# Scan rows of x and B: TensorE transposes replaced by VectorE 32x32 transposes and a round trip through DRAM

## The chip, the cores and the metric

The kernel runs on one core of one Trainium2 chip. The metric is device microseconds of one execution, from the first to the last instruction and what lies around them, as the median of the runs. Five engines work side by side, each with a queue of its own that it takes in order: TensorE (PE, with its weight loads PEld), VectorE (DVE), ScalarE (ACT), GpSimd (POOL) and SyncE (SP), which here only issues DMAs. ScalarE issues DMAs too; 16 DMA engines carry them all.

## The reference, cut to what matters

One step of a hybrid decoder layer for 336 tokens: 16 meta tokens, 256 prompt tokens and 8 sequences of 8 sample tokens.

```
h = rms_norm(x);  proj = h @ w_in                  # 2048 -> 18496 columns
xs, B, C = silu(conv4(proj[xBC]) + b)              # 4096 + 8*128 + 8*128 columns
dt = softplus(proj[dt] + dt_bias);  log_a = -dt * exp(a_log)
# per chunk of the scan, per group g of 8 heads:
cb   = C_i . B_j                                   # (i, j) tokens of a chunk
y    = sum_j cb * decay(i, j) * dt_j * x_j  +  C_i . h * exp(acum_i)
h    = exp(acum_end) * h + sum_j (to_end_j * dt_j * x_j) B_j
y = group_rms_norm((y + d_skip * xs) * silu(z)) @ w_ssd_out
# beside it a gated short convolution; both gated, @ w_o, + x, rms_norm
```

The scan contracts over tokens, so x and B are needed with tokens on the partitions ("rows"), while the projection and the conv leave them with channels on the partitions and tokens along them.

## The kernel before

All matmuls of the projections run as three products of a split: a weight block of 128x1024 is loaded on SyncE's queue (L92), ScalarE rounds it into `whi` (L94), VectorE makes the rest `wlo` (L96), and TensorE takes 8 steps of `whi` against both halves of the activations (L111, L112) and 8 of `wlo` against the upper half (L115). That is 24 matmuls a block; a unit (`unit`, `proj`) is two blocks into one bank of `pj`. Loads, `whi` and `wlo` have three buffers each, `pj` and `ms` banks two.

After the first part (norm, short convolution) the eight groups of the scan follow. While group g is scanned, the weight units of its neighbours are run, and the scan is woven between them: `weave` runs the units in the order z of g (four units), out projection of g−1 (eight units of one block), conv of g+1 (six units), and after each unit takes as many of the 23 steps of the generator `ssd(g)` as its share of the work. So each group has a z stage, an out stage (gate units in group 0 and at the end) and a conv stage, and the end of one conv stage is the start of the next z stage. A scheduler then fixes the order within each engine's queue from the program and its own estimates. It also hands out eight DMA semaphores in turn, over both queues, and lets a DMA wait until the holder before it has landed.

`conv_tile` evacuates a unit on ScalarE (`pad`, L462, L463), starts the conv there (L469), continues on VectorE (L471, three steps), takes the tanh on ScalarE (`cth`, L474) and writes the tile on VectorE (L475, L476): B (`BT`), C (`CT`) and four tiles of x (`xs`), in that order. `cacc` has two buffers.

In `ssd`, `rows(c)` for the three chunks (128, 128 and 80 tokens) makes the rows on TensorE: four transposes of `xs` and one of `BT` against the identity into two `ms` banks, and C.B of the chunk as one matmul in fp32 (recorded as two). VectorE multiplies the x rows by dt (`xdt`, L539), ScalarE and VectorE split the B rows (`bt`, L546, L547), VectorE masks C.B (`cbm`, L551). `decay(c)` makes the decay matrix in `W` (loaded from DRAM by L527), `weights(c)` multiplies it by `cbm` and makes `xe` on GpSimd (L568), `halve(c)` splits `xe`, `state(c)` is the update of the running state on TensorE (L585). The sample part updates `h` from the banks that L713 fills (VectorE, L716), and the group's normalising (`ms_r`, `ys`, `yh`, `yl`; L700 to L728) falls into the conv stage.

```
S = [{} for _ in range(NG)]
for _ in conv_units(0, S[0]):
    pass
for g in range(NG):
    parts = [(z_units(g, S[g]), 4, 2)]
    ...
    weave(parts, ssd(g, S[g]))
```

## Time and profile before

| | us |
|---|---|
| median of 3 runs | 1823.98 (1823.73 to 1824.63) |
| profiled execution, its own time | 1824.75 |
| its span, first to last instruction | 1823.0 |
| PE busy | 1814.9 |
| DVE busy | 1147.7 |
| ACT busy | 828.8 |
| POOL busy | 389.4 |
| granted TensorE clock | 1.00 |

A row of the timeline is: start, length, engine, line, operation, out<-in, shapes, count, and in brackets the idle time before it and what ended it. Neighbouring equal rows are merged. Matmuls overlap, so their cost is read from start to start. The view of a line or tile gives the shortest, median and longest duration in ns. A DMA issue appears as a row of the issuing queue (SPq, ACTq) and does not count as busy.

### The profile page before, as it was taken

The page shows a single profiled execution, that of the slowest core. Times are in us where ns is not written, and L with a number is a line of the kernel's source. Part 1 is how long each engine was busy: PE and PEld are TensorE (multiplying, and loading weights), DVE is VectorE, ACT ScalarE, POOL GpSimd, SP SyncE. Part 2 cuts the span into 40 slices and gives each one's busy share as a digit, 9 for nine tenths or more (in the row PEclk, how much of TensorE's full clock was granted, in tenths as well). Part 3 has the DMA queues.
Part 4 walks back from the last instruction along what each step waited for, and adds up shares of the span by engine and source line. Part 5 has one row for each costly group of instructions (what it writes and reads, how often), then busy time and mean ns, then how long its engine had stood idle before and what let it go on. Part 6 is the DMA issues. An engine that isn't in the chain of part 4 may idle for free.

```text
span 1823.0 us, 32410 instructions
## 1 busy us (share of the span) xinstructions
PE 1814.9 (100%) x13006; PEld 1798.0 (99%) x13006; DVE 1147.7 (63%) x1696; ACT 828.8 (45%) x1269; POOL 389.4 (21%) x398
## 2 busy tenths in 40 slices
PE   9999999999999999999999999999999999999998
PEld 9999999999999999999999999999999999999998
DVE  7745544444543335668587787877778777776544
ACT  6433333333333334645656354564546545343543
POOL 0000000000000001253162433524334252400012
PEclk9999999999999999999999999999999999999999
DMA  7444444444444446457566574665656657476553
GB/s 254 146 151 150 150 149 149 145 152 151 156 152 159 160 162 227 149 178 240 163 201 223 177 246 150 208 215 178 238 157 211 206 169 249 153 243 213 184 175 129
DMA packets 117286, 331.33 MB, mean 182 GB/s; under 512 B 20944, under 2 KB 37904, under 8 KB 117136
## 3 DMA queue, kind: packets, MB, share of 16 engines
q1 hardware_dynamic: 116272, 327.89, 55.9%
q8 instruction: 102, 1.67, 0.4%
q10 hardware_dynamic: 864, 1.38, 0.2%
q14 instruction: 48, 0.39, 0.1%
HBM read 296.34 MB, written 32.88 MB: 181 GB/s over the span
## 4 chain that ended last, share of the span: by engine, by line
PE 96%; DMA 2%; ACT 1%; DVE 1%; issue 0%; POOLq 0%; POOL 0%; SPq 0%; ACTq 0%; DVEq 0%
PE pj L111 30%; PE pj L112 30%; PE pj L115 29%; PE yb L650 2%; DMA wraw<-w 1%; PE ms L636 1%; PE pj L219 1%; PE yb L585 1%; PE pj L862 1%; ACT whi L94 0%; PE ms L534 0%; ACT W L559 0%; PE ms L219 0%; DMA ssms<-h 0%; PE yb L713 0%
## 5 line engine op out<-in xcount | busy, mean ns | idle before, releaser
L111 PE MATMUL pj<-hx,whi 128*128 128x320 f32 (+3 forms) x2880 | 864.4, 312 | 0.0
L112 PE MATMUL pj<-hx,whi 128*128 128x320 f32 (+3 forms) x2880 | 860.6, 311 | 0.0
L96 DVE TENSOR_TENSOR wlo<-wraw,whi 128x1024 fp32r<-128x1024 f32 x470 | 596.8, 1270 | 413.9 <-ACT whi L94 206.8
L94 ACT ACTIVATE whi<-wraw 128x1024 fp32r<-128x1024 f32 x470 | 496.7, 1057 | 768.0 <-PE pj L112 628.1
L111 PEld LDWEIGHTS pj<-hx,whi 128*128 128x128 f32 x2880 | 540.7, 188 | 4.6 <-ACT pad L462 1.7
L112 PEld LDWEIGHTS pj<-hx,whi 128*128 128x128 f32 x2880 | 541.5, 188 | 0.1
L115 PE MATMUL pj<-hx,wlo 128*128 128x320 f32 (+3 forms) x2880 | 485.4, 310 | 0.0
L115 PEld LDWEIGHTS pj<-hx,wlo 128*128 128x128 f32 x2880 | 440.6, 188 | 0.0
L111 PE MATMUL pj<-yh,whi 128*128 128x320 f32 x512 | 153.5, 311 | 1.2 <-ACT zs L503 0.9
L112 PE MATMUL pj<-yl,whi 128*128 128x320 f32 x512 | 152.3, 309 | 0.0
L596 POOL TENSOR_TENSOR h<-h,decS 128x512 f32<-128x512 f32 x64 | 76.4, 1227 | 147.5 <-PE ms L636 147.5
L111 PEld LDWEIGHTS pj<-yh,whi 128*128 128x128 f32 x512 | 96.2, 188 | 3.1 <-ACT zs L503 1.4
L112 PEld LDWEIGHTS pj<-yl,whi 128*128 128x128 f32 x512 | 96.3, 188 | 0.6
L115 PE MATMUL pj<-yh,wlo 128*128 128x320 f32 x512 | 95.8, 309 | 0.0
L242 POOL COPY SCS<-up 128x2 f32<-128x2 f32 x16 | 18.2, 1139 | 359.2 <-DVE up L236 329.0
L744 DVE TENSOR_TENSOR yan<-yan,pj 128x320 f32<-128x320 f32 x112 | 54.2, 485 | 62.9 <-PE pj L115 61.3
L471 DVE SCALAR_TENSOR_TENSOR cacc<-pad,V,cacc 128x360 f32<-128x360 f32 (+1 forms) x144 | 89.5, 621 | 2.0
L464 POOL COPY pad<-cs 128x24 f32<-128x24 f32 x48 | 56.2, 1172 | 126.6 <-DVE cacc L471 115.5
L115 PEld LDWEIGHTS pj<-yh,wlo 128*128 128x128 f32 x512 | 80.4, 188 | 0.0
L111 PE MATMUL pj<-vhi,whi 128*128 128x320 f32 x256 | 75.5, 308 | 0.0
L112 PE MATMUL pj<-vlo,whi 128*128 128x320 f32 x256 | 75.5, 308 | 0.0
L465 POOL COPY cs<-pad 128x3 f32<-128x3 f32 x48 | 45.0, 938 | 82.5 <-ACT pad L462 82.0
(286 smaller groups left out, 1721.7 us busy)
## 6 DMA issues: line engine op xcount, KB each, us to landing
wraw<-w SPq DMA_DIRECT2D x346, 512.0 KB, 3.9
wraw<-wso SPq DMA_DIRECT2D x64, 512.0 KB, 3.5
wraw<-wsc SPq DMA_DIRECT2D x32, 512.0 KB, 3.8
h<-h0T SPq DMA_DIRECT2D x32, 512.0 KB, 4.9
ssms<-h SPq DMA_DIRECT2D x32, 512.0 KB, 4.2
wraw<-wo SPq DMA_DIRECT2D x32, 512.0 KB, 3.9
xq_d<-xe SPq DMA_DIRECT2D x16, 320.0 KB, 3.4
W<-ac_d SPq DMA_DIRECT2D x8, 576.0 KB, 6.4
```

The source lines that it names most:

```text
L94: latest["act"] = nc.scalar.activation(hi[:, :n], raw[:, :n], AF.Copy).ins
L96: latest["dve"] = nc.vector.tensor_tensor(lo[:, :n], raw[:, :n], fb(hi[:, :n]), sub).ins
L111: nc.tensor.matmul(out, w, xh(k0 + k), start=first and k == 0, stop=False)
L112: nc.tensor.matmul(out, w, xl(k0 + k), start=False, stop=False)
L115: latest["pe"] = nc.tensor.matmul(out, w, xh(k0 + k), start=False, stop=last and k == nk - 1).ins
L219: nc.tensor.matmul(pu[i][:, :T - t0], w[:, o:o + P], x[:, k, t0:], start=k == 0 and j == 0, stop=k == 15 and j == 2)
L464: nc.gpsimd.tensor_copy(smp[:, :, 0:3], cs[:, 1:9, :])
L465: nc.gpsimd.tensor_copy(cs[:, 0, :], pad[:, 272:275])
L471: nc.vector.scalar_tensor_tensor(acc[:, i0:], pad[:, i0 + k:360 + k], col(V_CW, 4 * j + k), acc[:, i0:], mult, add)
L596: nc.gpsimd.tensor_tensor(split(h0[b]), split(h0[b]), bc(hv(decS[:, b, :], g), [P, 8, HP]), mult)
L650: nc.tensor.matmul(yb[q * HP:(q + 1) * HP, t, t0:t0 + n], x[:, h * HP:(h + 1) * HP], w[:, h, :], start=i == 0, stop=i == 3)
L744: nc.vector.tensor_tensor(ya[:, m, :TV], ya[:, m, :TV], pp[:, :TV], add)
```

## The change

The conv tile now also makes its rows. After a tile of B or x is written, VectorE transposes it in blocks of 32x32 (320 tokens, then the last 32) back into the tile's `cacc`. That leaves token 32b+q of channel block a on partition 32a+q. Four DMAs a tile, one for each 32 partitions, write it to DRAM (`xr_d`, two buffers by group) as rows by token: 32 x 11 pieces of 32 numbers each. They are put in a list and issued on ScalarE's queue (`flush`) after the first conv step of the next tile, or after the evacuation of the first z unit. `load(c)` reads the rows back with eight DMAs a group on SyncE's queue. `rows` is gone: C.B of the three chunks is made in one visit (`cross`), and `rows_in(c)` multiplies and splits the loaded rows. `decay(1)` comes a step earlier, `weights(0)` and `rows_in` a step later than `rows` and `weights(0)` stood.

The diff:

```diff
--- before.py
+++ after.py
@@ -28,6 +28,7 @@
 DUM = 14
 WARM = 10
 NSTEP = 23
+XR = 352
 
 C_ID, C_U, C_M1, C_UQ, C_M1Q, C_ONE = 0, 128, 272, 400, 480, 560
 C_SEG = 688
@@ -60,6 +61,7 @@
     sg_d = dr.tile([KT, P, TV], F32, name="sg_d")
     xq_d = [dr.tile([80, 4, 512], F32, name=f"xq_d{i}") for i in range(2)]
     bq_d = [dr.tile([80, 4, P], F32, name=f"bq_d{i}") for i in range(2)]
+    xr_d = [dr.tile([XR, 640], F32, name=f"xr_d{i}") for i in range(2)]
 
     V = keep.tile([P, V_ALL], F32, name="V")
     CR = keep.tile([P, C_ALL], F32R, name="CR")
@@ -454,7 +456,13 @@
         nc.gpsimd.memset(CZ, 0.0)
         czs = CZ.rearrange("p (s i w) -> p s i w", s=2, w=40)
 
-        def conv_tile(src, j, t0, out, cs):
+        pend = []
+
+        def flush():
+            while pend:
+                nc.scalar.dma_start(*pend.pop(0))
+
+        def conv_tile(src, j, t0, out, cs, rows=None):
             pp = proj(src, t0)
             pad = pads[npad[0] % 2]
             npad[0] += 1
@@ -467,6 +475,7 @@
             i0 = META if t0 else 0
             acc = pb.tile([P, 360], F32, name="cacc")
             nc.scalar.activation(acc[:, i0:], pad[:, i0:360], AF.Identity, bias=col(V_CB, j), scale=col(V_CW, 4 * j))
+            flush()
             for k in range(1, 4):
                 nc.vector.scalar_tensor_tensor(acc[:, i0:], pad[:, i0 + k:360 + k], col(V_CW, 4 * j + k),
                                                acc[:, i0:], mult, add)
@@ -477,19 +486,27 @@
                 out[:, 272:].rearrange("p (b t) -> p b t", t=8),
                 th[:, 272:360].rearrange("p (b t) -> p b t", t=11)[:, :, 3:11], 1.0,
                 acc[:, 272:360].rearrange("p (b t) -> p b t", t=11)[:, :, 3:11], add, mult)
+            if rows is not None:
+                nc.vector.transpose(acc[:, :320], out[:, :320])
+                nc.vector.transpose(acc[:, 320:XR], out[:, T - 32:])
+                to, c = rows
+                for a in range(0, P, 32):
+                    pend.append((to.rearrange("(b q) c -> q b c", q=32)[:, :, c + a:c + a + 32],
+                                 acc[a:a + 32, :XR].rearrange("p (b f) -> p b f", f=32)))
 
         def conv_units(g, st):
             cs = pb.tile([P, 6, 9, 3], F32, name="cs")
             nc.sync.dma_start(cs, convst[:, g])
+            to = xr_d[g % 2]
             BT = st["BT"] = pb.tile([P, T], F32, name="BT")
-            conv_tile(w1[64 + g], 32 + g, 0, BT, cs[:, 4])
+            conv_tile(w1[64 + g], 32 + g, 0, BT, cs[:, 4], (to, 512))
             yield
             CT = st["CT"] = pb.tile([P, T], F32, name="CT")
             conv_tile(w1[72 + g], 40 + g, 12, CT, cs[:, 5])
             yield
             xs = st["xs"] = pb.tile([P, 4, T], F32, name="xs", tag=f"xs{g % 2}", bufs=1)
             for t in range(4):
-                conv_tile(w1[32 + 4 * g + t], 4 * g + t, 0, xs[:, t, :], cs[:, t])
+                conv_tile(w1[32 + 4 * g + t], 4 * g + t, 0, xs[:, t, :], cs[:, t], (to, P * t))
                 yield
             nc.sync.dma_start(convo[:, g], cs)
 
@@ -501,6 +518,7 @@
                 th = pb.tile([P, 360], F32, name="cth", bufs=1)[:, :TV]
                 nc.scalar.activation(th, pz, AF.Tanh, scale=0.5)
                 nc.scalar.activation(z[:, :TV], pz, AF.Copy)
+                flush()
                 nc.vector.scalar_tensor_tensor(z[:, :TV], th, 1.0, z[:, :TV], add, mult)
                 st["zs"].append(z)
                 yield
@@ -518,7 +536,7 @@
             xw = free[:, :1024].rearrange("p (i n) -> p i n", n=512)
             h0, h0t = [], []
             ys = pb.tile([P, 4, T], F32, name="ys", bufs=1)
-            W, xdt, xe, bt, cbm, hst = ([None] * 3 for _ in range(6))
+            W, xdt, xe, cbm, hst = ([None] * 3 for _ in range(5))
             W[0], W[1] = (pb.tile([P, 8, PX], F32, name="W")[:, :, :n] for n in (P - META, PX))
             W[2] = pb.tile([P, 8, 80], F32, name="W2", bufs=1)
             E = pb.tile([P, 8, PX], F32, name="E", bufs=1)
@@ -527,29 +545,37 @@
                 nc.sync.dma_start(w[:r], ac_d[c][8 * g:8 * g + 8, :].partition_broadcast(r))
             NT, TGT = (P - META, PX, 80), (META, P, 2 * P)
 
-            def rows(c):
-                (t0, n), m = CH[c], NT[c]
-                pp = ps.tile([P, 512], F32, name="ms")
-                for t in range(4):
-                    nc.tensor.transpose(pp[:n, t * P:t * P + P], xs[:, t, t0:t0 + n], ident)
+            bt = [pb.tile([P, 2, P], F32R, name="bh0", bufs=1), free[:, 1024:1280].rearrange("p (i n) -> p i n", n=P),
+                  pb.tile([P, P], F32, name="bt", bufs=1)]
+
+            def load(c):
+                xdt[c] = big("xdt", 3)
+                b = bt[c] if c == 2 else fb(bt[c][:, 1, :])
+                rows = xr_d[g % 2]
+                for o, r, n in ((0, P * c, P),) if c < 2 else ((0, 256, 64), (64, 336, 16)):
+                    nc.sync.dma_start(xdt[c][o:o + n], rows[r:r + n, :512])
+                    nc.sync.dma_start(b[o:o + n], rows[r:r + n, 512:])
+
+            def cross():
                 pq = ps.tile([P, 512], F32, name="ms")
-                nc.tensor.transpose(pq[:n, 0:P], BT[:, t0:t0 + n], ident)
-                nc.tensor.matmul(pq[:n, P:P + m], BT[:, t0:t0 + n], CT[:, TGT[c]:TGT[c] + m], start=True, stop=True)
-                xdt[c] = big("xdt", 3)
-                nc.vector.tensor_tensor(split(xdt[c][:n]), split(pp[:n]), bc(hv(dtt[:n, c, :], g), [n, 8, HP]), mult)
-                if c == 2:
-                    bt[c] = pb.tile([P, P], F32, name="bt", bufs=1)
-                    nc.scalar.activation(bt[c][:n], pq[:n, 0:P], AF.Copy)
-                else:
-                    bt[c] = (free[:, 1024:1280].rearrange("p (i n) -> p i n", n=P) if c else
-                             pb.tile([P, 2, P], F32R, name="bh0", bufs=1))
-                    nc.scalar.activation(bt[c][:, 0, :], pq[:, 0:P], AF.Copy)
-                    nc.vector.tensor_tensor(bt[c][:, 1, :], pq[:, 0:P], fb(bt[c][:, 0, :]), sub)
-                cbm[c] = pb.tile([P, PX], F32, name="cbm")
-                u0 = META if c == 0 else 0
-                for a, b, o in ((0, m, 0),) if c < 2 else ((META, 80, 0), (0, META, 64)):
-                    nc.vector.tensor_tensor(cbm[c][:n, o:o + b - a], pq[:n, P + a:P + b],
-                                            U[:, u0 + a:u0 + b] if c < 2 else UQ[:, a:b], mult)
+                qs = [pq[:n, o:o + m] for o, m, (_, n) in zip((0, NT[0], NT[0] + NT[1]), NT, CH)]
+                for c, (t0, n) in enumerate(CH):
+                    nc.tensor.matmul(qs[c], BT[:, t0:t0 + n], CT[:, TGT[c]:TGT[c] + NT[c]], start=True, stop=True)
+                for c, (_, n) in enumerate(CH):
+                    m = NT[c]
+                    cbm[c] = pb.tile([P, m], F32, name=f"cbm{c}", bufs=1)
+                    u0 = META if c == 0 else 0
+                    for a, b, to in ((0, m, 0),) if c < 2 else ((META, 80, 0), (0, META, 64)):
+                        nc.vector.tensor_tensor(cbm[c][:n, to:to + b - a], qs[c][:, a:b],
+                                                U[:, u0 + a:u0 + b] if c < 2 else UQ[:, a:b], mult)
+
+            def rows_in(c):
+                n = CH[c][1]
+                nc.vector.tensor_tensor(split(xdt[c][:n]), split(xdt[c][:n]), bc(hv(dtt[:n, c, :], g), [n, 8, HP]), mult)
+                if c < 2:
+                    b = fb(bt[c][:, 1, :])
+                    nc.scalar.activation(bt[c][:, 0, :], b, AF.Copy)
+                    nc.vector.tensor_tensor(bt[c][:, 1, :], b, fb(bt[c][:, 0, :]), sub)
 
             def decay(c):
                 n, m, w = CH[c][1], NT[c], W[c]
@@ -596,30 +622,33 @@
                     nc.gpsimd.tensor_tensor(split(h0[b]), split(h0[b]), bc(hv(decS[:, b, :], g), [P, 8, HP]), mult)
 
             yield
-            rows(0)
+            cross()
             yield
             decay(0)
             yield
             nc.scalar.activation(E, W[1], AF.Exp)
-            rows(1)
             for u in range(4):
                 h = pb.tile([P, 2, 512], F32, name="h0", bufs=4)
                 nc.sync.dma_start(h, h0T[g, :, 2 * u:2 * u + 2, :])
                 h0 += [h[:, 0, :], h[:, 1, :]]
                 h0t.append(h)
             yield
+            decay(1)
+            for c in range(3):
+                load(c)
+            yield
+            rows_in(0)
             weights(0)
             yield
             halve(0)
-            decay(1)
-            yield
-            rows(2)
+            rows_in(1)
             yield
             carry(0)
             state(0, pieces(0))
             weights(1)
             yield
             halve(1)
+            rows_in(2)
             decay(2)
             yield
             carry(1)
```

Three places show what the change moves. The first is TensorE's queue around the first of the three visits of a group (group 3); before, two more such visits follow in the next weight blocks, with chunk 1 and chunk 2. `ms` is the bank, `CR` holds the identity. Before:

```order
L115 MATMUL pj<-hx,wlo 128x320 x8
L534 MATMUL ms<-CR,xs 128x128 x4
L536 MATMUL ms<-CR,BT 128x128
L537 MATMUL ms<-CT,BT 128x112
L111 MATMUL pj<-hx,whi 128x320
```

TensorE's queue at the same place now, where the only visit of the group stands:

```order
L117 MATMUL pj<-hx,wlo 128x320 x8
L563 MATMUL ms<-CT,BT 128x112
L563 MATMUL ms<-CT,BT 128x144
L563 MATMUL ms<-CT,BT 80x80
L113 MATMUL pj<-hx,whi 128x320
```

The transposes are gone, and the three C.B matmuls stand together; the two later visits are gone.

The second is ScalarE's queue from the last conv tile of the same stage into the first z unit (`cth<-pj` and `zs<-pj` are the z unit's evacuation, `cacc<-pad` the conv's first step, `whi` the splits). Before:

```order
L94 ACTIVATE whi<-wraw 128x1024
L462 ACTIVATE pad_6710<-pj 128x272
L463 ACTIVATE pad_6710<-pj 128x8x8
L469 ACTIVATE cacc<-pad_6710,V 128x360
L94 ACTIVATE whi<-wraw 128x1024
L474 ACTIVATE cth<-cacc 128x360
L94 ACTIVATE whi<-wraw 128x1024
L502 ACTIVATE cth<-pj 128x320
L503 ACTIVATE zs<-pj 128x320
L562 ACTIVATE W<-W 128x8x112
```

ScalarE's queue at this place now (`xr_d<-cacc` is one of the four writes of a tile):

```order
L477 ACTIVATE cacc<-pad_6712,V 128x360
L463 DMA xr_d_75<-cacc 32x11x32 x2
L96 ACTIVATE whi<-wraw 128x1024
L483 ACTIVATE cth<-cacc 128x360
L96 ACTIVATE whi<-wraw 128x1024
L463 DMA xr_d_75<-cacc 32x11x32
L519 ACTIVATE cth<-pj 128x320
L520 ACTIVATE zs<-pj 128x320
L463 DMA xr_d_75<-cacc 32x11x32 x3
L96 ACTIVATE whi<-wraw 128x1024 x3
```

Two splits that stood ahead of the z unit's evacuation now stand behind it, with the last tile's four writes around it (one ahead, three behind; the two at the top are the tile's before). The first of these four waits for that tile's transposes on VectorE.

The third is VectorE's queue in the same conv stage, from the state updates (`h`) to the first `wlo` of the last conv tile. Before:

```order
L726 SCALAR_TENSOR_TENSOR ys<-ys,V,ms_r 128x320
L728 TENSOR_TENSOR yl<-ys,yh 128x320
L475 SCALAR_TENSOR_TENSOR xs<-cth,cacc 128x272
L476 SCALAR_TENSOR_TENSOR xs<-cth,cacc 128x64
L728 TENSOR_TENSOR yl<-ys,yh 128x320
L726 SCALAR_TENSOR_TENSOR ys<-ys,V,ms_r 128x320 x2
L96 TENSOR_TENSOR wlo<-wraw,whi 128x1024
```

VectorE's queue at this place now (`cacc<-xs` are the transposes):

```order
L755 SCALAR_TENSOR_TENSOR ys<-ys,V,ms_r 128x320 x2
L484 SCALAR_TENSOR_TENSOR xs<-cth,cacc 128x272
L485 SCALAR_TENSOR_TENSOR xs<-cth,cacc 128x64
L757 TENSOR_TENSOR yl<-ys,yh 128x320
L490 STREAM_TRANSPOSE cacc<-xs 128x320
L491 STREAM_TRANSPOSE cacc<-xs 128x32
L757 TENSOR_TENSOR yl<-ys,yh 128x320
L755 SCALAR_TENSOR_TENSOR ys<-ys,V,ms_r 128x320 x2
L98 TENSOR_TENSOR wlo<-wraw,whi 128x1024 x2
```

One pair of transposes stands in the piece shown; another pair, of the tile before, stands some rows ahead of it in the same run.

## The prediction

> **What bounds the kernel now.** I read the page first, then the stages, then single instructions.
>
> ```profile
> span 1823.0 us, 32410 instructions
> PE 1814.9 (100%) x13006; PEld 1798.0 (99%) x13006; DVE 1147.7 (63%) x1696; ACT 828.8 (45%) x1269; POOL 389.4 (21%) x398
> PE 96%; DMA 2%; ACT 1%; DVE 1%; issue 0%; POOLq 0%; POOL 0%; SPq 0%; ACTq 0%; DVEq 0%
> ```
>
> TensorE is busy for 1814.9 of 1823.0 us and carries 96% of the chain that ended last. The view of the waits says the same from the other side: this is nearly all that TensorE waited for in the groups, while SyncE stands for 1070.3 us until VectorE frees a weight buffer, so the loads run ahead.
>
> ```profile
> PE pj L111 <- ACT zs L503: 0.9, 1, 0.9
> SPq L92 <- DVE wlo L96: 1070.3, 406, 9.1
> ```
>
> So a matmul taken away is time taken away, as long as the split weights (whi from ScalarE, wlo from VectorE) still come ahead of it. How far the suppliers are from their limit differs by stage. Here is group 3: the conv units, the z units, the first out units (columns: length, then busy time of PE, PEld, DVE, ACT, POOL, granted clock, share of the DMA engines, GB/s).
>
> ```profile
> 1033.70:1072.20 38.50, 38.50 (x254) 37.52 (x252) 32.86 (x55) 24.37 (x42) 17.83 (x20) 1.00 0.66 214
> 1072.20:1102.20 30.00, 30.00 (x212) 29.99 (x209) 22.99 (x36) 19.14 (x34) 8.74 (x7) 1.00 0.76 250
> 1102.20:1137.70 35.50, 35.50 (x334) 34.72 (x332) 24.18 (x36) 13.16 (x23) 9.43 (x7) 1.00 0.48 150
> ```
>
> The conv stage is the tight one (VectorE 85%, ScalarE 63%), and it is there that the change puts its new work. The clock is 1.00 throughout and plays no part.
>
> **What leaves TensorE.** The timeline of one visit; each L115 row is the end of a weight block.
>
> ```profile
> 1081.69 1.32 PE L115 MATMUL pj<-hx,wlo 128*128 128x320 f32 x8
> ...
> 1085.18 1.33 PE L115 MATMUL pj<-hx,wlo 128*128 128x320 f32 x8
> 1086.35 0.60 PE L534 MATMUL ms<-CR,xs 128*128 128x128 f32 x4
> 1086.78 0.27 PE L536 MATMUL ms<-CR,BT 128*128 128x128 f32 x1
> 1086.89 0.37 PE L537 MATMUL ms<-CT,BT 128*128 128x112 f32 x2
> ...
> 1089.47 1.32 PE L115 MATMUL pj<-hx,wlo 128*128 128x320 f32 x8
> ```
>
> A block without a visit takes 1085.18 − 1081.69 = 3.49 us, the one with it 1089.47 − 1085.18 = 4.29: a visit costs 0.80. Of that the five transposes are 1086.89 − 1086.35 = 0.54; 0.26 are the C.B matmul and the turn from and to the weight blocks. All 15 transposes of a group go: 3 x 0.54 = 1.62. The three C.B matmuls stay but share one turn; I put the two turns saved at 0.1 each, between nothing and 0.26. Together 1.6 to 2.1, and I take 1.81 a group, over 8 groups 14.5 us. That is all the gain there is, since ScalarE and VectorE are not the bound.
>
> **What VectorE gets.** Two transposes a tile, 320 and 32 wide, five tiles a group. The profile has the operation at 256.
>
> ```profile
> L643 DVE STREAM_TRANSPOSE xe<-xe 128x256 f32<-128x256 f32 x8 | 3.6, 446 | 0.3
> ```
>
> By width, 446 ns become some 0.5 for the pair, 0.7 when each has a fixed part; I take 0.55. The place where this decides is the first weight block of the last conv tile. VectorE works there without a pause from 1050.86 on, with the normalising of the group before and the state updates, and its wlo ends at 1065.69, 1.04 us before TensorE wants it:
>
> ```profile
> 1050.86 0.49 DVE L701 TENSOR_SCALAR ms_x<-ms 128x320 f32<-128x320 f32 x1 [1.11 <-ACT ms_r L700]
> 1064.47 1.22 DVE L96 TENSOR_TENSOR wlo<-wraw,whi 128x1024 fp32r<-128x1024 f32 x1
> 1066.73 0.46 PE L115 MATMUL pj<-hx,wlo 128*128 128x336 f32 x2
> ```
>
> In the new order two pairs stand in that run: 2 x 0.55 = 1.1 against 1.04. About 0.1 us of waiting for TensorE, with bounds 0 and 0.4.
>
> **What ScalarE gets.** Four DMA issues a tile, 160 in all. An issue is not counted as busy but holds the queue. The trace has no ScalarE issue with 32x11x32 pieces; nearest are SyncE's writes from SBUF to DRAM in three dimensions.
>
> ```profile
> L669 SPq DMA_DIRECT2D xq_d<-xe x16: 311/382/445, 806.9 to 1583.7; - x16
> L670 SPq DMA_DIRECT2D bq_d<-bhh x16: 593/598/1338, 796.3 to 1568.9; - x16
> ```
>
> Bounds 0.31 and 1.34; I take the median of the first, 0.38, because its pieces are also partitions by blocks. The order matters more than the sum. Before, ScalarE splits the second block of the second z unit already at 1076.01, and TensorE wants it at 1082.85:
>
> ```profile
> 1076.01 1.04 ACT L94 ACTIVATE whi<-wraw 128x1024 fp32r<-128x1024 f32 x1
> 1080.06 0.50 ACT L474 ACTIVATE cth<-cacc 128x360 f32<-128x360 f32 x1 [3.01 <-DVE cacc L471]
> 1080.47 1.04 ACT L94 ACTIVATE whi<-wraw 128x1024 fp32r<-128x1024 f32 x1
> 1081.78 0.44 ACT L502 ACTIVATE cth<-pj 128x320 f32<-128x320 f32 x1 [0.26 <-DVE xs L476]
> 1082.11 0.43 ACT L503 ACTIVATE zs<-pj 128x320 f32<-128x320 f32 x1
> 1082.85 0.30 PE L111 MATMUL pj<-hx,whi 128*128 128x320 f32 x1
> ```
>
> Now this split stands behind the first write of the last conv tile, which waits for that tile's transposes, behind cth and zs of the first z unit, and behind three more writes. When are the transposes done? VectorE's rows before them:
>
> ```profile
> 1071.77 0.50 PE L713 MATMUL yb<-xh,bh 32*128 32x512 f32 x4
> 1076.14 0.62 DVE L471 SCALAR_TENSOR_TENSOR cacc<-pad,V,cacc 128x360 f32<-128x360 f32 x1
> ...
> 1079.95 1.21 DVE L96 TENSOR_TENSOR wlo<-wraw,whi 128x1024 fp32r<-128x1024 f32 x1
> 1081.09 0.43 DVE L475 SCALAR_TENSOR_TENSOR xs<-cth,cacc 128x272 f32<-128x272 f32 x1
> 1081.45 0.22 DVE L476 SCALAR_TENSOR_TENSOR xs<-cth,cacc 128x64 f32<-128x64 f32 x1
> 1081.58 1.58 DVE L561 TENSOR_SCALAR W<-W,act 128x112 f32<-128x112 f32 x8
> ```
>
> From the conv's first step to the end of the tile are 1081.58 − 1076.14 = 5.44 us, two state updates and one wlo among them. In the new order a second wlo (1081.09 − 1079.95 = 1.14) and the transposes (0.55) come on top: 7.1 us. They start no earlier than L713 has filled the bank (about 1072.2) and not before the wlo ahead of them, which by the two pairs is late by a microsecond too (about 1073.1). I take the later one: transposes done at 1080.2. Then one issue 0.38, cth and zs 0.66 (by their starts), three issues 1.14, the split 1.05: whi is ready at 1083.4, 0.6 after TensorE wants it. With the 0.1 from above and 0.1 for the hops between engines: 0.8 us lost in each of the seven conv stages that run beside a group, 5.6 us. With an issue of 0.31 and the earlier start it is nothing; each further 0.1 us of issue adds 0.4.
>
> **What the DMA engines and SyncE get.** A write is 352 packets of 128 bytes, 20 writes a group are 7040. The window 929.5 to 930.5, where only 448-byte packets of W move, prices small packets from one side, the page's mean packet from the other:
>
> ```profile
> DMA packets 533, 0.24 MB, mean 238 GB/s; under 512 B 533, under 2 KB 533, under 8 KB 533
> q1 hardware_dynamic: 533, 0.24, 82.2%
> q1 hardware_dynamic: 116272, 327.89, 55.9%
> ac_d<-acx SPq DMA_DIRECT2D x1, 4.0 KB, 1.7
> ```
>
> 0.822 x 16 / 533 = 25 ns a packet, or 0.559 x 16 x 1823 / 116272 = 140 ns. By the first, nearest in size, a group's writes take 7040 x 25 / 16 = 11 us of the engines, most of it in the conv stage, which goes from 0.66 to about 0.9. I count it as hidden, with the weight loads up to a microsecond later. In the built program all DMAs take eight semaphores in turn, and each waits until the holder before it has landed, on whichever queue that was: some weight loads now wait for a ScalarE write, and some ScalarE issues for a load. The smallest landing in the trace, 1.7 us in the row above, is less than the lead of the splits (1082.85 − 1077.05 = 5.8 us at the block above); I price it at nothing and keep a microsecond a stage for the upper end. The eight row reads move 0.84 MB a group, at 238 GB/s 3.5 us, in the z stage with 30 x 0.24 = 7 us free. Their issues, 8 x 0.38 to 0.6 us, and their waits for ScalarE's last write lie in front of weight loads on SyncE's queue; the 1070 us above are the cover. rows_in needs them before the first state matmul, six blocks (6 x 3.49 = 21 us) after the C.B visit, and only two POOL steps and one of ScalarE lie between, the longest of them this:
>
> ```profile
> L574 POOL TENSOR_TENSOR xw<-xe,xw x16: 1286/1801/1944, 757.1 to 1556.8; 128x512 fp32r<-128x512 f32 x16
> ```
>
> No wait there. decay(1) one step earlier and weights(0) one later keep all their instructions on the same engines, and one small ScalarE copy goes: nothing. One buffer for each cbm is free since the group before: nothing.
>
> **The sum.** 1823.0 − 14.5 + 5.6 = 1814.1 of span. The profiled execution took 1824.75, 1.75 more than its span, and is 0.77 above the median of 1823.98: 1814.1 + 1.75 − 0.77 = 1815.1. A run-to-run change below 0.2% (3.6 us) cannot be told from none.
>
> **The rivals.**
> - *All is hidden.* The lost time per stage stays under 0.3 us: 1809.5 to 1812. For it: ScalarE's rows above have gaps of 3.01 us. Against it: the 1.04 us. Chance 0.15.
> - *The suppliers eat the gain.* 1.5 to 2.6 us a stage, which an issue of 0.56 to 0.83 us would make (0.8 + 4 x the surplus over 0.38): 1820 to 1827.6, around 1824, no change that can be told. For it: bq_d's 0.598. Chance 0.19.
> - *ScalarE's queue becomes the bound: slower.* Four issues in a row block cth and every split behind them. The gain is used up at 14.5 / 7 = 2.07 us a stage, an issue of 0.7; past 0.83 it is slower by 0.2%. At 1.0 us a stage loses 0.8 + 4 x 0.62 = 3.3: 1824 − 14.5 + 23 = 1832. For it: 1338 ns, the longest bq_d issue, and that a write has 352 pieces; against it: the medians. Chance 0.17.
> - *Small writes are slow in the DMA engines.* At 140 ns a packet the writes of a group take 62 us. The engines have 38.5 x 0.34 + 30 x 0.24 + 35.5 x 0.52 = 39 us free in these three stages: 23 us over, seven times, about 1970. Against it: 64 pieces of 64 bytes landed in DRAM in 1.7 us. Chance 0.04. The Trainium skill, "DMA: Bandwidth & Descriptors", section Specifications, speaks for this rival: below 512 B a transfer is not at line rate, and the engine reads, modifies and writes. The 448-byte packets above show no such price, but they are reads from DRAM.
>
> That the transposes stay is excluded by the order shown above the prediction.
>
> **The numbers.** The forecast, 0.3 to 1.5 us lost a stage, 1812 to 1820, has 0.45. Faster 0.45 + 0.15 = 0.60, the same 0.19, slower 0.17 + 0.04 = 0.21. The range is 1809 (all hidden) to 1829 (into the third rival); most of the slower cases, and little else, lie outside.
>
> **What would show it.** Right: TensorE has 120 matmuls fewer; one visit a group; ScalarE's issues near 0.4 us each; in the waits TensorE shows L113 behind whi or zs for some 6 us in all, at the second block of the second z unit. Wrong: issues of 0.7 us or more, TensorE's waits summing to over 14 us, or waits behind a weight load (DMA 1.0 busy in the conv stage); wrong on the other side: no wait at all, and a span of 1808.5.

## The result and the profile after

The changed kernel takes 1885.3 us (1881.92 to 1888.12), the one before 1823.86 in the same rounds: 1.0335 times as long, 95% interval 1.0318 to 1.0353. That is 61 us slower, where 9 us faster was forecast, and outside the range.

The page of the profiled execution (1881.92 us), its span and its engines:

```profile
span 1880.1 us, 32572 instructions
PE 1822.3 (97%) x12886; PEld 1795.3 (95%) x12886; DVE 1190.4 (63%) x1776; ACT 826.5 (44%) x1261; POOL 377.4 (20%) x398
```

The 120 matmuls are gone (12886 against 13006), and yet TensorE is busy 7.4 us longer, in a span 57.1 us longer. The waits of TensorE, which came to little before, show most of it (releaser, us in total, times, longest):

```profile
PE pj L113 <- ACT whi L96: 24.2, 18, 3.4
PE pj L113 <- DVE yan L773: 18.5, 6, 3.5
PE pj L113 <- ACT zs L520: 7.6, 6, 1.4
```

Together 50.3 us, 49.1 more than before. The longer busy time is the clock. Around one of the long waits, in two windows (length, then PE, PEld, DVE, ACT, POOL, granted clock, DMA share, GB/s):

```profile
1243.50:1247.30 3.80, 0.40 (x3) 0.14 (x1) 3.80 (x6) 1.77 (x3) 0.28 (x1) 0.84 0.58 155
1247.30:1252.80 5.50, 5.46 (x20) 5.47 (x21) 2.00 (x3) 0.00 (x0) 2.42 (x1) 0.50 0.51 179
```

TensorE stands still, and when it goes on it has half the clock for some 5 us. Over the execution the mean granted clock is 0.993: 0.007 x 1880 = 13.2 us. That is an upper figure, since a little of the lost clock falls into the waits themselves (0.16 x 3.8 = 0.6 us in the first window). So 49.1 of waits and at most 13.2 of clock stand against a gain of 12.2 (the span of the run with the gain alone, below, is 1810.8): at most 50.1 of the 57.1 us. The remaining 7 or more are not assigned to a row.

Where do the waits start? SyncE's queue, by releaser, shows what is new:

```profile
SPq L94 <- DVE wlo L98: 984.1, 388, 9.1
SPq L556 <- DMA xr_d<-cacc: 45.7, 8, 8.3
SPq L557 <- DMA xr_d<-cacc: 38.8, 10, 5.0
SPq L545 <- PE yb L742: 26.8, 7, 4.2
```

The row reads (L556, L557) stand 84.5 us on the queue until writes on ScalarE's queue have landed, and the read of W (L545) 26.8 us until TensorE's last state matmuls are done. The wait for VectorE, the cover that the prediction counted on, is still there with 984.1 of its 1070.3 us. Here is the place where the row reads stand in one group, at the turn from the conv stage to the z stage:

```profile
1210.39 3.92 SPq L94 DMA_DIRECT2D wraw<-w  x3
1214.40 0.91 SPq L632 DMA_DIRECT2D h<-h0T  x2
1218.02 0.33 SPq L499 DMA_DIRECT2D cs<-convst  x1
1223.26 0.33 SPq L556 DMA_DIRECT2D xdt<-xr_d  x1
1223.64 0.42 SPq L94 DMA_DIRECT2D wraw<-w  x1
```

From 1214.31 to 1223.64, 9.3 us, no weight load is issued; TensorE takes a block in 3.5. The last 4.9 us of them (1218.35 to 1223.26) are the wait of the first row read. ScalarE then waits for the loads, 5.40 us for this one and 2.27 for the next, and only then comes to the decay matrix behind them (`W`, 2.55 us from 1232.92 on):

```profile
1228.62 1.06 ACT L96 ACTIVATE whi<-wraw 128x1024 fp32r<-128x1024 f32 x1 [5.40 <-DMA wraw<-w]
```

VectorE's queue at the start of the out stage shows the second place. TensorE needs the first evacuation there (`yan`, which empties a bank of the out projection; L744 before, L773 now). Before, the third chunk's `xdt` stood behind it, and TensorE waited 0.3 us for these evacuations in all:

```profile
1105.11 1.07 DVE L744 TENSOR_TENSOR yan<-yan,pj 128x320 f32<-128x320 f32 x2
1106.12 0.69 DVE L539 TENSOR_TENSOR xdt<-ms,dtt 80x512 f32<-80x512 f32 x1
```

Now:

```profile
1239.48 1.79 DVE L574 TENSOR_TENSOR xdt<-xdt,dtt 128x512 f32<-128x512 f32 x1
1241.20 0.28 DVE L578 TENSOR_TENSOR xw<-xw 128x128 fp32r<-128x128 f32 x1
1241.40 2.08 DVE L98 TENSOR_TENSOR wlo<-wraw,whi 128x1024 fp32r<-128x1024 f32 x1
1243.40 1.35 DVE L592 TENSOR_TENSOR W<-W,cbm 128x1152 f32<-128x1152 f32 x1
1244.67 1.21 DVE L98 TENSOR_TENSOR wlo<-wraw,whi 128x1024 fp32r<-128x1024 f32 x1
1245.80 0.48 DVE L522 SCALAR_TENSOR_TENSOR zs<-cth,zs 128x320 f32<-128x320 f32 x1
1246.21 0.68 DVE L574 TENSOR_TENSOR xdt<-xdt,dtt 80x512 f32<-80x512 f32 x1
1246.81 0.87 DVE L773 TENSOR_TENSOR yan<-yan,pj 128x320 f32<-128x320 f32 x2
```

```profile
1247.34 0.64 PE L113 MATMUL pj<-yh,whi 128*128 128x320 f32 x1 [3.43 <-DVE yan L773]
```

VectorE is never idle from 1239.48 on, and the bank that TensorE wants is emptied at 1247.3. This is the 3.43 us wait of the window above, and five groups have it at 3.43 to 3.45. The third chunk's `xdt` now stands ahead of the evacuation. The second chunk's takes 1.79 us, with its operand in SBUF and GpSimd's `xw` beside it (1238.90 to 1240.72); before, with the operand in a bank, it took 0.69 (1099.49). All eight groups now have it at 1.78 to 1.81.

The prices that the prediction had to bound: one write's issue on ScalarE's queue (min/median/max), and one pair of transposes:

```profile
L463 ACTq DMA_DIRECT2D xr_d<-cacc x160: 309/426/1230, 707.6 to 1580.7; - x160
```

```profile
1213.88 0.50 DVE L490 STREAM_TRANSPOSE cacc<-xs 128x320 f32<-128x320 f32 x1
1214.30 0.16 DVE L491 STREAM_TRANSPOSE cacc<-xs 128x32 f32<-128x32 f32 x1
```

An issue is 0.426 us (taken: 0.38), a pair is 0.58 from its first start to its last end (taken: 0.55), and a write has landed after 4.6 us in the median (1.8 to 9.7). The page gives the writes' queue 59744 packets in 2.7% of the 16 engines' span: 0.027 x 16 x 1880.1 / 59744 = 13.6 ns a packet (bounds taken: 25 and 140). None of these is where the time went.

### The profile page after: what moved, and what is told of

It is laid out like the page before. It is cut to its first block, busy times and chain, and to the rows that moved or that the text cites. A ratio compares the mean times of both kernels' runs of the same rounds, so it can differ in the third digit from the quotient of the medians.

```text
span 1880.1 us, 32572 instructions
## 1 busy us (share of the span) xinstructions
PE 1822.3 (97%) x12886; PEld 1795.3 (95%) x12886; DVE 1190.4 (63%) x1776; ACT 826.5 (44%) x1261; POOL 377.4 (20%) x398
## 3 DMA queue, kind: packets, MB, share of 16 engines
q10 hardware_dynamic: 59744, 8.60, 2.7%
## 5 line engine op out<-in xcount | busy, mean ns | idle before, releaser
L113 PE MATMUL pj<-yh,whi 128*128 128x320 f32 x512 | 158.2, 320 | 31.3 <-DVE yan L773 18.5
L773 DVE TENSOR_TENSOR yan<-yan,pj 128x320 f32<-128x320 f32 x112 | 53.9, 485 | 69.9 <-PE pj L117 68.4
L472 POOL COPY pad<-cs 128x24 f32<-128x24 f32 x48 | 42.2, 880 | 146.1 <-DVE cacc L480 125.0
L483 ACT ACTIVATE cth<-cacc 128x360 f32<-128x360 f32 (+1 forms) x48 | 24.1, 503 | 106.3 <-DVE cacc L480 83.0
```

The lines of the kernel that those rows point to most:

```text
L113: nc.tensor.matmul(out, w, xh(k0 + k), start=first and k == 0, stop=False)
L472: nc.gpsimd.tensor_copy(smp[:, :, 0:3], cs[:, 1:9, :])
L483: nc.scalar.activation(th[:, i0:], acc[:, i0:], AF.Tanh)
L773: nc.vector.tensor_tensor(ya[:, m, :TV], ya[:, m, :TV], pp[:, :TV], add)
```

## The experiments

Theory 1: the row reads on SyncE's queue hold back weight loads. Theory 2: ScalarE's 160 issues and the writes' traffic do it (the forecast's own mechanism, stronger). Theory 3: the new order of the steps and VectorE's added work bunch the evacuations. All runs stand against a run of the kernel before on the same chip, 1823.4 to 1824.2 us.

**A ladder from the gain alone to the change.** Four kernels take the change apart, each with one thing more. None has reads:

```diff
-                    nc.sync.dma_start(xdt[c][o:o + n], rows[r:r + n, :512])
-                    nc.sync.dma_start(b[o:o + n], rows[r:r + n, 512:])
+                    nc.gpsimd.memset(xdt[c][o:o + n], 0.0)
+                    nc.gpsimd.memset(b[o:o + n], 0.0)
```

The first three have no writes (nothing is put in the list that `flush` issues). The gain alone:

> The gain alone: TensorE's 120 transposes are left out and C.B is made in one visit, no writes, no reads, no transposes on VectorE (zeros by GpSimd in place of the rows), with the rows' steps where they stood before. My sum of the gain, 14.5 us: 1808 to 1811. If a part of it is less than I took (the visit for C.B measured 0.56 us a group, 12.3 to 13.3 us over the traces so far): 1810 to 1813. The transposes on VectorE are the difference to the run at 1818.8 us.

Then the transposes back in:

> As the run without writes and reads (1833 us, 23.5 above 1823.9 less 14.5; zeros in place of the rows), but with the multiplications of the rows, decay(1) and weights(0) put back into the steps where they stood before; the only visit for C.B stays. Theory 3 (these steps put 3.4 us of work ahead of VectorE's first evacuations of the out stage, TensorE waits 16.3 us for them in all and runs at a lower clock after it): 1808 to 1813 us, no wait behind the evacuations of over 0.5. If the 23.5 us come from the transposes on VectorE in the conv stage: 1828 to 1834.

Then the steps of the change:

> The rows' writes to DRAM and their reads are both left out: the loaded tiles are filled with zeros by GpSimd, so x and B of the scan are wrong, and all else stays: 120 matmuls fewer, the transposes on VectorE, the multiplications of the rows, the new order of the steps. Theory 1 (row reads on SyncE's queue stand in front of weight loads while they wait for ScalarE's writes to land): the waits of TensorE go, 1809 to 1816 us. Theory 2 (ScalarE's 160 issues and the writes' traffic hold up the splits): the same, 1809 to 1816. Theory 3 (the new order of the steps and the transposes on VectorE bunch the work at the end of the z stage): the waits stay, 1870 to 1885.

Then the writes:

> Only the reads are left out (zeros by GpSimd instead); the 160 writes stay on ScalarE's queue. SyncE's queue has the same order but for the reads. Theory 1: the long waits at the end of the z stage go, what is left is what ScalarE's issues cost, 1812 to 1825 us. Theory 2: little changes, 1860 to 1885. Theory 3: 1870 to 1885.

| kernel | us | ratio to before (95%) | step, us |
|---|---|---|---|
| gain alone | 1813.12 | 0.9942 (0.9927 to 0.9957) | -10.3 |
| + transposes on VectorE | 1818.79 | 0.9977 (0.9965 to 0.9989) | +5.7 |
| + the new order of the steps | 1833.08 | 1.0057 (1.0039 to 1.0076) | +14.3 |
| + four writes a tile on ScalarE's queue | 1849.69 | 1.0141 (1.0125 to 1.0156) | +16.6 |
| + eight reads a group on SyncE's queue (the change) | 1885.30 | 1.0335 (1.0318 to 1.0353) | +35.6 |

Only the first two rungs are faster than before. The gain is 10.3 us and not 14.5; 1813.12 is just over both ranges of its expectation. The third and the fourth kernel came out between the ranges of the theories, so none of the theories holds alone. The order of the steps costs 14.3 us with no DMA of the rows in the kernel at all: theory 3 is right for that part, and its wait is this row of the kernel without writes and reads,

```profile
PE pj L113 <- DVE yan L772: 16.3, 7, 3.4
```

which with the old steps is down to 1.7 us in two waits. The 1818.79 missed its expectation by 6 us; the transposes in the conv stage, with the shift of SyncE's order that came with them (in the same group three weight loads ahead of the read of W in place of four), are the larger part of that (5.7). The two were not told apart. Theories 1 and 2 have no place in a kernel without the rows' DMAs (1809 to 1816), and it took 1833.

**The reads.** On GpSimd's queue instead of SyncE's, whose order is otherwise kept:

```diff
-                    nc.sync.dma_start(xdt[c][o:o + n], rows[r:r + n, :512])
-                    nc.sync.dma_start(b[o:o + n], rows[r:r + n, 512:])
+                    nc.gpsimd.dma_start(xdt[c][o:o + n], rows[r:r + n, :512])
+                    nc.gpsimd.dma_start(b[o:o + n], rows[r:r + n, 512:])
```

> The eight row reads of a group go to GpSimd's queue, nothing else; SyncE's queue keeps its order. Theory 1: weight loads are no longer behind the reads, the waits of TensorE fall from 50 us to under 15, 1813 to 1832 us; if GpSimd's own DMAs land late or block its xe step, up to 1850. Theory 2 and theory 3: 1875 to 1890.

Measured: 1855.29 us, 1.0176 (1.0161 to 1.0192). The same bytes and the same waits, off SyncE's queue, cost 5.6 us over no reads in place of 35.6. It came out over the range; writes and steps, which stayed in, already take 1849.69.

The reads left on SyncE, and only two weight loads put in front of them:

```diff
+                        tc.add_manual_dep(ins, hold[-1].name, mybir.DependencyInfo(mybir.DependencyClass.NoSync,
+                                                                                   mybir.DependencyReason.DATA), reason="row")
```

(`ins` is each read, `hold[-1]` the last weight load of the z units.)

> The change as it is, with one order: the eight row reads of a group are held on SyncE's queue behind the last two weight loads of the z units, which stood among and behind them. The same DMAs, the same waits of the reads. Theory 1 (weight loads late because they stand behind reads that wait): the two loads come some 4 us earlier, TensorE's waits at the end of the z stage shrink, 1850 to 1870 us. If the reads cost by their traffic or by late rows: 1878 to 1890.

Measured: 1853.21 us, 1.0154 (1.0137 to 1.0171): 32 us less than the change for two loads moved in one queue. SyncE's queue at the same place of that kernel:

```profile
1199.68 3.92 SPq L94 DMA_DIRECT2D wraw<-w  x3
...
1210.08 2.96 SPq L94 DMA_DIRECT2D wraw<-w  x2
1213.37 0.33 SPq L557 DMA_DIRECT2D xdt<-xr_d  x1
```

The gap from the three loads to the next is 1210.08 - 1203.60 = 6.5 us in place of 9.3, and the reads stand 14.4 us for DMAs in all, in place of 84.5. Theory 1 is shown, for 30 to 32 of the 35.6 us: the price of the reads' place in SyncE's queue, with all that hangs on it. ScalarE's queue differs too: `cth` waits 23.3 us there for writes to land in the change, 10.9 with the writes and no reads, and 3.6 in each of these two kernels. What ties these waits to the reads was not tested.

In what form? Here the reads take rows that landed long ago, at nearly the same places of SyncE's queue (a further edit, not shown, holds each read behind the last load of `h`, to keep its place):

```diff
-                rows = xr_d[g % 2]
+                rows = xr_d[(g + 1) % 2 if g else 0]
```

> The reads stay on SyncE's queue at nearly the same places, with the same bytes, but read the buffer of the group before, which landed long ago, so that they wait for no write of this group (rows of x and B are the wrong group's). Theory 1 with the wait as the cost: 1815 to 1830 us. If the reads cost by their issues and their 0.84 MB a group in the busy DMA engines and not by the wait: 1855 to 1885. Theory 2 and theory 3: 1870 to 1885.

Measured: 1881.35 us, 1.0317 (1.0300 to 1.0334), against my expectation for theory 1 and inside the range for cost by traffic. Traffic is excluded as the main cost by the two runs before, which move the same bytes for 1855 and 1853. The reads' waits fit:

```profile
SPq L559 <- DMA wraw<-w: 31.2, 14, 3.8
SPq L559 <- DMA xr_d<-cacc: 26.4, 12, 4.6
```

They need no write of this group any more, and still stand 57.6 us for DMAs: for weight loads and for writes whose semaphore they take over. So the rows' own dependence is not needed to block the queue: here a read waits for whichever DMA had its semaphore before. How the 84.5 us of the change divide between the two is not told apart.

**The writes.** Does ScalarE's queue cost the 16.6 us? In the kernel with the writes, SyncE's order in the conv stage is another one: two weight loads, then the read of W, the last writes of the sample states (ssms), then three loads. In the kernel without writes and reads three loads stand ahead of W, in the kernel before four. Without the writes, then with them:

```profile
1177.14 5.40 SPq L94 DMA_DIRECT2D wraw<-w  x3
...
1184.92 0.42 SPq L544 DMA_DIRECT2D W<-ac_d  x1
1186.05 1.97 SPq L747 DMA_DIRECT2D ssms<-h  x2
1188.13 1.53 SPq L94 DMA_DIRECT2D wraw<-w  x2
```

```profile
1187.49 1.44 SPq L94 DMA_DIRECT2D wraw<-w  x2
1193.18 0.33 SPq L545 DMA_DIRECT2D W<-ac_d  x1
1195.06 1.47 SPq L748 DMA_DIRECT2D ssms<-h  x2
...
1197.21 3.83 SPq L94 DMA_DIRECT2D wraw<-w  x3
```

I gave the kernel without writes and reads the second order:

```diff
+        if hold["n"] == hold.get("at"):
+            for a in hold["ins"]:
+                tc.add_manual_dep(ld, a.name, mybir.DependencyInfo(mybir.DependencyClass.NoSync,
+                                                                   mybir.DependencyReason.DATA), reason="order")
```

(`ld` is the second weight load after the start of a group's steps, `hold["ins"]` the W read and the last ssms write.)

> Again no writes and no reads (zeros in place of the rows). The third, fourth and fifth weight load of the z units are held in SyncE's order behind the W read, which waits for TensorE's last state matmuls, and behind the last two ssms writes, which wait for VectorE's h: the order that SyncE's queue has where the writes are in. Theory 2a (the 16.6 us that the writes cost come from this order and not from ScalarE): 1845 to 1852 us with TensorE waiting 10 to 16 us behind whi in the conv and z stages. Theory 2b (ScalarE's issues and the writes' traffic): 1831 to 1836, as without the order.

Measured: 1847.78 us, 1.0134 (1.0119 to 1.0149), 14.7 more than without that order and 1.9 less than with the writes. TensorE's waits behind whi, without a write and then with them (without that order they were 0.3 us):

```profile
PE pj L118 <- ACT whi L101: 17.2, 7, 3.1
```

```profile
PE pj L113 <- ACT whi L96: 14.0, 8, 2.5
```

The wait behind whi, which the forecast put down to ScalarE's issues, is there at the same size with no issue on ScalarE at all. Theory 2 is not needed for this wait: the order of the weight loads alone makes one of its size. A small part for ScalarE's issues is not excluded. In the kernel with the writes the split that TensorE waits for starts at 1205.41, right behind the last write's issue, which ends at 1205.37.

The writes priced without that order, on GpSimd's queue:

> The run at 1818.8 us (no reads, zeros in place of the rows, the steps where they stood before) with the writes added on GpSimd's queue. It prices the writes' traffic and their hold on cacc, without ScalarE's queue: if the traffic is hidden, 1818 to 1822 us; if 7040 packets of 128 bytes a group cost the weight loads time, 1826 to 1845.

Measured: 1830.91 us, 1.0038 (1.0025 to 1.0051), 12.1 more than 1818.79. So the writes are not free either, even off ScalarE's queue; TensorE then waits 11.6 us behind zs (L520), and 3.3 without them. Traffic, GpSimd's blocked queue and the small shifts of order are not told apart here. That part stays open. The 14.7 and the 12.1 can't be added: the writes as the change has them, with the order that comes with them, cost 16.6 in all.

**Repairs.** Writes and reads both on GpSimd's queue, steps of the change:

> Writes and reads of the rows both on GpSimd's queue; the steps as in the change. SyncE's queue then has the third weight load of the z units ahead of the W read again. If what the change loses is SyncE's order, its blocked queue and ScalarE's issues, only the 23.5 us of the steps' order stay and a few for GpSimd's blocked queue: 1832 to 1842 us. If the writes' traffic in the DMA engines is what costs: 1850 to 1858, as with the reads alone on GpSimd.

Measured: 1843.62 us, 1.0109 (1.0092 to 1.0126), just over the first range; TensorE's waits behind whi are down to 0.7 us, those behind yan are 16.3. To shorten VectorE's run there, the multiplication by dt was moved to GpSimd, then half of the B rows' split as well:

```diff
-                nc.vector.tensor_tensor(split(xdt[c][:n]), split(xdt[c][:n]), bc(hv(dtt[:n, c, :], g), [n, 8, HP]), mult)
+                nc.gpsimd.tensor_tensor(split(xdt[c][:n]), split(xdt[c][:n]), bc(hv(dtt[:n, c, :], g), [n, 8, HP]), mult)
```

> Writes and reads on GpSimd's queue as in the run at 1843.6, and the rows' multiplication by dt on GpSimd too (its operand is in SBUF now). That takes 3.1 us (0.68, 1.79 and 0.68) out of VectorE's run ahead of the first evacuations of the out stage, where TensorE waits 2.3 to 3.7 us a group. Theory 3: these waits go and the clock's drops behind them, 1818 to 1826 us. If GpSimd's later xe or its sharing with VectorE gives it back: 1832 to 1845.

> As the run before, with the second half of the B rows' split on GpSimd as well (0.28 to 1.1 us a chunk of VectorE). Theory 3: 1 to 3 us less than that run, 1816 to 1825 us; if GpSimd is now too late for the state matmuls: 1825 to 1845.

Measured: 1849.27 us, 1.0141 (1.0126 to 1.0156), and 1852.94, 1.0161 (1.0146 to 1.0176): both slower than 1843.62 and over all ranges of their expectations. VectorE and GpSimd in the first of them:

```profile
1221.48 3.32 DVE L98 TENSOR_TENSOR wlo<-wraw,whi 128x1024 fp32r<-128x1024 f32 x1
...
1226.83 1.21 DVE L98 TENSOR_TENSOR wlo<-wraw,whi 128x1024 fp32r<-128x1024 f32 x1
```

```profile
1221.37 1.09 POOL L574 TENSOR_TENSOR xdt<-xdt,dtt 80x512 f32<-80x512 f32 x1
1222.42 1.29 POOL L600 TENSOR_TENSOR xw<-xe,xw 128x512 fp32r<-128x512 f32 x1
1223.79 1.91 POOL L594 TENSOR_TENSOR xe<-xdt,tet 80x512 f32<-80x512 f32 x1
```

While GpSimd works without a pause from 1221.4 to 1225.7, a wlo takes 3.32 us; after it, at 1226.83, the same takes 1.21. What was taken from VectorE came back as longer instructions beside GpSimd: TensorE's waits behind yan are 19.4 us in place of 16.3. The Trainium skill, "SBUF — State Buffer", section Who interferes with whom, has the rule: a VectorE instruction with two inputs in SBUF contends with a GpSimd instruction that reads SBUF. The rows agree, with 3.32 against 1.21 us.

The decay matrices' multiplication by C.B needs no rows and can go ahead of them, which shortens VectorE's run without GpSimd. Tried three times, with DMAs on GpSimd's queue and 24 steps, the same with 23, and that with the reads on SyncE behind the last weight loads:

```diff
+            wmult(1)
+            yield
             rows_in(0)
             weights(0)
```

> Writes and reads on GpSimd's queue, and the steps rearranged: the decay matrices are multiplied by C.B ahead of the rows, in the z stage, since they need no rows; the rows' multiplications come after; 24 steps. Theory 3: the waits behind the evacuations go, 1810 to 1820 us, faster than before. If the rows land too late for it or GpSimd's queue holds up the conv: 1822 to 1840.

> Writes and reads on GpSimd's queue as in the run at 1843.6, 23 steps, SyncE's order as there; the decay matrices of chunks 0 and 1 are multiplied by C.B in the z stage, ahead of the rows, and the rows' steps stand one step later. That takes the multiplications of 1.08 and 1.35 us, and the third chunk's 0.68, out of the run ahead of VectorE's first evacuations of the out stage. Theory 3: the waits there (16.3 us) fall to under 5 and the clock's drops go, 1816 to 1826 us. If the rest of that run, slowed by GpSimd beside it, still holds the evacuations: 1832 to 1844.

> As the first of these three, with the reads on SyncE's queue instead, behind the last weight loads of the z units. Theory 1: the reads' waits now only stand in front of the out stage's weight loads, which have slack there; 1816 to 1832 us, within 6 us of the first. If the reads' waits still make weight loads late: 1835 to 1855.

Measured: 1864.68 us, 1.0230 (1.0215 to 1.0245); 1834.75, 1.0051 (1.0034 to 1.0068); 1841.46, 1.0091 (1.0076 to 1.0106). The first missed both its ranges, the other two came out in the range of their second case. In the first, SyncE's queue stands again: the loads of `h` 68.0 us for the writes of ssms, the read of W 25.7, and TensorE waits 19.4 us behind wlo. The second, which has nearly the same edits without the extra step, is the fastest changed kernel that computes all. In its profiled execution (1841.09 us, its slowest) TensorE waits 9.8 us behind zs and 8.5 behind yan: the wait behind yan is halved from 16.3, and one behind zs has come up in front of it. None of the repairs is as fast as the kernel before.

## Why the prediction was wrong

- **"The 1070 us above are the cover"** is the step that failed, with 30 to 32 of the 61 us. The number is a sum over 406 loads of the whole kernel, and 984.1 us of it are still there in the changed one. At the turn from the conv to the z stage, where the reads stand, the queue has no such lead: they stand 84.5 us in all, in one group no weight load is issued for 9.3 us, and a split then waits 5.40 us for DMA. The row was read as if the cover were where it was needed.
- **The semaphores, priced "at nothing":** the run with the old rows shows the reads waiting 57.6 us for DMAs whose data they don't need. I compared the wait with the lead of one block, not with what the queue holds behind the waiting DMA.
- **"decay(1) one step earlier and weights(0) one later ... nothing":** 14.3 us, measured without any DMA of the rows. The instructions were counted, and not what they then stand in front of: the evacuations of the out stage, for which TensorE has two banks. Nor do all keep their length: the second chunk's `xdt` went from 0.69 to 1.79 us.
- **The splits behind ScalarE's writes, 5.6 us:** the wait came at about the place that the forecast named, 14.0 us in the kernel with the writes alone. That the place fits is luck in good part, since SyncE's order without a single write gives 17.2. The prediction read the order of ScalarE and VectorE and not that of the queue that feeds both.
- **"The clock ... plays no part":** true of the kernel before, and up to 13.2 us of the changed one, as the price of its waits.
- **The gain, 14.5 us:** 10.3 by the medians, 12.2 by the spans. The transposes on VectorE, put at 0.1 us a stage, cost 5.7 in all, with the shift of SyncE's order that came with them.
- **Right:** the price of an issue (0.426 for 0.38), of a pair of transposes (0.58 for 0.55), 120 matmuls fewer. The pair is partly luck: by width, 446 ns become 0.446 x 352 / 256 = 0.61 and not "some 0.5". The reads' 0.84 MB are 336 rows of 2560 bytes, 0.86; nothing hangs on that. The prediction's own sign of being wrong, waits over 14 us in sum, came with 50.3, but without issues of 0.7 us.
- **The rivals:** the third had the sign; by its own rule (slower from an issue of 0.83 us on) 0.426 would have been faster, so its mechanism is not what happened. The fourth fell: 13.6 ns a packet and not 140. Per byte the small packets are slow, though: the profile's page has 8.60 MB in 59744 packets for that queue, 144 bytes in 13.6 ns or 10.6 GB/s of an engine, where the page of before has 327.89 MB in 116272 packets for SyncE's queue, 2820 bytes in 140 ns or 20 GB/s. The rule set beside this rival in the prediction (the Trainium skill, "DMA: Bandwidth & Descriptors", Specifications: below 512 B a transfer is not at line rate) agrees with that. The price is far from what the rival needed.

## What to carry to other kernels

Look for the cover at the place where it is needed: a sum of waits over the kernel says nothing of the one stage where the queue is already late. Where a change adds a DMA that waits, list what stands behind it on its queue, and look at the order of every queue that feeds the bound engine, the scheduler's own shifts too. Then test the order by itself: a kernel with the DMAs left out, and one with only the order imposed, told more here than any price of an instruction.

## What the runs showed of the hardware

After a wait TensorE can run at half its clock for a stretch of 3.4 us or two, and a wait shorter than such a stretch can be enough. In the kernel with the writes alone, the clock was half from 1206.2 to 1209.6, at the end of a wait of 2.45 us and behind it. In the change it was half from 1246.1 to 1252.9, two such stretches, around a wait of 3.43. In the kernel without writes and reads a wait of 3.45 us was not followed by it (the first and the last of these, each with the wait's row, then the window behind it; the granted clock is third from the end):

```profile
1206.52 0.64 PE L113 MATMUL pj<-hx,whi 128*128 128x320 f32 x1 [2.45 <-ACT whi L96]
1206.30:1209.60 3.30, 3.08 (x11) 3.08 (x12) 3.10 (x10) 3.00 (x4) 0.00 (x0) 0.50 1.09 342
```

```profile
1446.48 0.42 PE L113 MATMUL pj<-yh,whi 128*128 128x320 f32 x1 [3.45 <-DVE yan L772]
1446.50:1450.00 3.50, 3.50 (x24) 3.50 (x25) 1.95 (x3) 0.28 (x1) 2.37 (x1) 1.00 0.60 206
```

A stretch filled with matmuls costs about 1.5 us: by their starts they are 0.27 us apart in it and 0.15 behind it, 3.4 x (1 - 0.15 / 0.27). The Trainium skill, "TensorE: Matmul & The Clock Gate", Part 1, tells of half the clock after an idle window of about 3.4 us. The slow stretch is of that length here too, but a wait that was enough is shorter than that window, with 2.45 us.
